# Stick-breaking logits: the second product from the high part of q alone, 64 rows in one of two row tiles

## The chip, the cores and the metric

One Trainium2 chip, one of its cores. The metric is the time of one execution of the program on the device, in microseconds; for the kernel before it is the median of three runs.

## What is computed

A decoder trunk of two layers over 512 tokens of width 1024. In each layer a SwiGLU half step, a mixing step (eight stick-breaking heads, eight forgetting heads, four memory heads, each branch gated), and another SwiGLU half step, each between RMS norms. The change touches the logits of the stick-breaking heads:

```python
def _stick_breaking_attention(q, k, v):          # 8 heads of 64, 512 tokens, blocks of 128 queries
    ...
        z = jnp.einsum('bhqd,bhkd->bhqk', qb, k).astype(jnp.float32) * scale
        mask = key_pos[None, :] < q_pos[:, None]
        log_beta = jax.nn.log_sigmoid(z)
        log_not = jnp.where(mask, log_beta - z, 0.0)
        log_between = lax.cumsum(log_not, axis=3, reverse=True) - log_not
        w = jnp.where(mask, jnp.exp(log_beta + log_between), 0.0)
        return jnp.einsum('bhqk,bhkd->bhqd', w.astype(v.dtype), v)
```

## The kernel before

Every product is done with operands that are split in two: a high part in TensorE's reduced 32-bit format (`F32R`) and a low part, the remainder. A full product takes three matmuls (`mm3`: high by high, high by low, low by high). `split(h, l, src)` writes the high part with ScalarE and the low part with VectorE.

The program writes its order out by hand. A queue `Q` holds the jobs of the dense products (projections, gates, branch outputs, each with its weights' loads), and `Q.weave` puts their steps between the parts of an attention head: a head is a generator that yields ("pe", us) after a part's matmuls and ("wait", us) where its next part should come only after so much other TensorE work.

A stick head is `stick_head` (L1174). Heads come in pairs: pair `p` has its q and k in one projection of 128 rows, head 0 on rows 0 to 63, head 1 on rows 64 to 127. `HEAD_ROWS` gives for each the rows `r` that are its own, the other half `ro`, and its index j:

```python
HEAD_ROWS = ((slice(0, HD), slice(HD, P), 0), (slice(HD, P), slice(0, HD), 1))
```

`proj` (L1374) makes the tiles. For q it is `[128, 2, 512]`: plane j has on rows `r` the high part of head j and on rows `ro` its low part. For the k of a stick head (`twice`) it is `[128, 4, 512]`: plane j has the high part of k on both halves, plane 2 + j the low part on both halves; GpSimd copies them from `r` to `ro` (L1390). So one matmul of 128 rows with plane j of both gives high by high plus low by high, and a second one, plane j of q with plane 2 + j of k, gives high by low plus low by low.

The head does this for query blocks i = 3, 2, 1, 0 of 128 queries, with 512, 384, 256 and 256 keys: block 3 in one PSUM bank, block 2 in another, blocks 1 and 0 together in a third (tag `z`, four banks). For each block both matmuls (L1183) stand one behind the other. Then ScalarE (L1188 to L1190: abs, exp, log) and VectorE (L1191, a scan at L1196, L1197) make the weights, ScalarE the last exponential (L1198). After a planned wait of 13 us of other TensorE work `transposed` (L1158) turns the weights with ten transposes and splits them, and `attend` (L1144) multiplies by v. There are 8 such heads in each of 2 layers.

Forgetting heads (`fox_head`, `fox_pre`) use the same `proj` with other shapes; their q stays `[128, 2, 512]`. Tiles of the tag `q` have two buffers.

Of the kernel before, what the change touches and what calls it, by code (L numbers as in the profile page):

```python
# [18 lines left out]
P = 128  # L19
# [4 lines left out]
def kernel(  # L24
# [38 lines left out]
    nc = tc.nc  # L63
    _, S, D = x.shape
    M = mem.shape[1]
    L = w_in.shape[0]
    NT = S // P
# [5 lines left out]
    HEAD_ROWS = ((slice(0, HD), slice(HD, P), 0), (slice(HD, P), slice(0, HD), 1))  # L73
# [25 lines left out]
    def tmp(name):  # L99
        return sb.tile([P, S], F32, tag="f32t", bufs=5, name=name)  # L100
# [3 lines left out]
    def stile(shape, tag, name, dt=F32R):  # L104
        return sb.tile(shape, dt, tag=tag, bufs=BUFS[tag], name=name)

    def blk(tag, name):
        return stile([P, 2, S], tag, name)

    def pbank(tag, name):  # L110
        return ps.tile([P, S], F32, tag=tag, bufs=4, name=name)
# [67 lines left out]
    def split(h_ap, l_ap, src, scale=None, later=False):  # L179

        if scale is None:
            both = [nc.scalar.copy(h_ap, src)]  # L182
            make = lambda: nc.vector.tensor_tensor(l_ap, src, h_ap.bitcast(F32), ALU.subtract)  # L183
        else:
            both = [nc.scalar.activation(h_ap, src, AF.Copy, scale=scale)]  # L185
            make = lambda: nc.vector.scalar_tensor_tensor(l_ap, src, scale, h_ap.bitcast(F32), ALU.mult, ALU.subtract)  # L186
        if later:
            return make
        both.append(make())
        if Q.pinned:  # L190
            for ins in both:
                tc.keep_in_program_order(ins)
        return both
# [16 lines left out]
    def gemm(pt, units, m, act, ks=None):  # L210

        last = sum(un.nk for un in units) - 1
        for un in units:
            for k in range(un.nk):
                kk = un.k0 + k
                if ks is not None and kk not in ks:
                    continue
                c = slice(m * P, (m + 1) * P)
                ah, al = act(kk)
                mm3(pt, un.h[:, k, c], un.l[:, k, c], ah, al, kk == 0, kk == last)  # L220
                yield 3 * pt.shape[1] * PE_US
# [914 lines left out]
    def attend(pv, j, vts, pj, tri, ot, name):  # L1136

        r, rl, _ = HEAD_ROWS[j]
        for kt in reversed(range(NT)):
            lo = QLO[kt]  # L1140
            v = vts[kt // 2][:, 2 * (kt % 2) + pj, 2 * j:2 * j + 2, :].rearrange("p e c -> p (e c)")
            for part in range(2):
                tc.keep_in_program_order(
                    nc.tensor.matmul(pv[:, lo:], v, tri_part(tri, part, kt, kt * P - lo), start=(kt == NT - 1 and part == 0),  # L1144
                                     stop=(kt == 0 and part == 1), skip_group_check=True))
        s = tmp("s" + name)
        nc.scalar.copy(s[r], pv[rl])
        nc.vector.tensor_tensor(s[r], pv[r], s[r], ALU.add)
        split(ot[r, 0], ot[r, 1], s[r])

    def transposed(ptile, name):

        tri = tri_tile("pt" + name)
        for kt in reversed(range(NT)):
            pt = pbank("z", f"pt{name}_{kt}")
            for i in range(kt, NT):
                tc.keep_in_program_order(
                    nc.tensor.transpose(pt[:, i * P:(i + 1) * P], ptile[i][:, kt * P:(kt + 1) * P], ident[:]))  # L1158
            split(tri_part(tri, 0, kt), tri_part(tri, 1, kt), pt[:, kt * P:].rearrange("p (a b) -> p a b", b=P))
        return tri  # L1160
# [12 lines left out]

    def stick_head(q, k, vts, pj, j, cut, ot, name):  # L1174

        ptile = {}
        for rows in ((3,), (2,), (1, 0)):
            pz = pbank("z", f"z{name}_{rows[0]}")
            w0 = (rows[0] + 1) * P
            for i in rows:  # L1180
                o = pz[:, (rows[0] - i) * 2 * P:][:, :max((i + 1) * P, 2 * P)]
                for kk in (j, 2 + j):
                    nc.tensor.matmul(o, q[:, j, i * P:(i + 1) * P], k[:, kk, :o.shape[1]], start=(i == rows[0] and kk == j),  # L1183
                                     stop=(kk == 2 + j), skip_group_check=True)
            w = w0 + (len(rows) - 1) * P
            zr, t = pz[:, :w], tmp(f"t{name}_{rows[0]}")

            nc.scalar.activation(t[:, :w], zr, AF.Abs)  # L1188
            nc.scalar.activation(t[:, :w], t[:, :w], AF.Exp, scale=-1.0)
            nc.scalar.activation(t[:, :w], t[:, :w], AF.Ln, bias=one_t[:])  # L1190
            nc.vector.scalar_tensor_tensor(t[:, :w], zr, 0.0, t[:, :w], ALU.max, ALU.add)  # L1191
            if len(rows) > 1:
                nc.vector.memset(t[:, w0 - 1:w0], 1e30)
            c1 = CUT if len(rows) > 1 else CUT - P
            back, fac = t[:, w - 1::-1], cut[:, c1 - w:c1][:, ::-1]
            nc.vector.tensor_tensor_scan(back, fac, back, 1e30, ALU.mult, ALU.add)  # L1196
            nc.vector.tensor_tensor(t[:, :w], zr, t[:, :w], ALU.subtract)  # L1197
            nc.scalar.activation(t[:, :w], t[:, :w], AF.Exp)  # L1198
            for i in rows:
                c = (rows[0] - i) * 2 * P  # L1200
                ptile[i] = t[:, c:c + (i + 1) * P]
        yield ("pe", 1.4)
        yield ("wait", W_SB0)
        wt = transposed(ptile, name)
        yield ("pe", 1.1)
        yield ("wait", W_SB1)
        attend(pbank("mm", "pv" + name), j, vts, pj, wt, ot, name)
        yield ("pe", 1.2)
# [120 lines left out]
    def mixing(l, src, ks, vs, rest, dst):  # L1329
# [5 lines left out]
        st, marks = {}, {}  # L1335
# [38 lines left out]
        def proj(key, un, scale):  # L1374
            nm = f"{key[0]}{l}_{key[1]}_{key[2]}"
            pt = pbank("mm", "p" + nm)
            yield from gemm(pt[:], [un], 0, act)
            if key[0] == "q":

                t = st[key] = blk("q", nm)  # L1380
                for r, ro, j in HEAD_ROWS:
                    split(t[r, j], t[ro, j], pt[r], scale=scale)
            else:

                twice = key[1] == 0
                t = st[key] = stile([P, 4 if twice else 3, S], "k", nm)
                for r, ro, j in HEAD_ROWS:
                    split(t[r, j], t[r, 2 + j if twice else 2], pt[r])
                    if twice:
                        nc.gpsimd.tensor_copy(t[ro, j::2], t[r, j::2])  # L1390
                    else:
                        nc.gpsimd.tensor_copy(t[ro, j], t[r, j])
# [12 lines left out]
        def project(br, p):  # L1405
            base = br * 1536
            marks["before", br, p] = len(Q.jobs)
            for x, off, scale in (("q", 0, 0.125), ("k", 512, None)):
                un1 = Unit(w_in[l], 0, ND, base + off + p * P, P, f"{x}{l}_{br}_{p}")
                marks[br, p] = Q.add([un1], lambda x=x, un1=un1, scale=scale: proj((x, br, p), un1, scale))  # L1410
                if (br, p, x) == (1, FOX[0], "k"):
                    Q.add([], lambda: forget_cumsum(l, st["fl"], st))
# [94 lines left out]
        def run():  # L1507
# [32 lines left out]
            def stick(p, j):  # L1540
                return stick_head(st["q", 0, p], st["k", 0, p], st["v", 0, p // 2], p % 2, j, st["cut"], st["o", 0][p],
                                  f"s{l}_{p}_{j}")
# [141 lines left out]
    for l in LAYERS:  # L1684
        i, mn = 3 * l, []
# [43 lines left out]
```

## Time and profile before

| | |
|---|---|
| median of three runs | 2349.4 us (2349.32 to 2351.5) |
| span of the profiled execution | 2349.9 us (first to last instruction; the page gives no other time of it) |
| TensorE products, busy | 2337.9 us (99%), 11623 matmuls |
| TensorE weight loads, busy | 1977.6 us (84%) |
| VectorE, ScalarE, GpSimd busy | 1799.9, 1506.5, 75.5 us |
| granted TensorE clock | 1.000 |
| stick heads | from 435.6 to 635.5 us, and from 1601.2 to 1800.9 us |

In the rows of the profile, PE is TensorE's products, PEld its weight loads, DVE is VectorE, ACT ScalarE, POOL GpSimd. L1183 is line 1183 of the kernel. A row of a timeline gives start, duration, engine, line, operation, what is written and read, the shape of the array used and of the moving operand; neighbours of one line are merged (x8), and the shape shown is the first one's. Matmuls are pipelined: the duration of one reaches over the start of the next, so distances are taken between starts.

### The profile page before, as it was taken

To read this page: it belongs to the slowest core of one execution; us is meant where nothing else is said; L and a number is where in the kernel's file an instruction comes from. 1 tells how busy PE (TensorE), PEld (TensorE's weight loads), DVE (VectorE), ACT (ScalarE), POOL (GpSimd) and SP (SyncE) were. 2 spreads that over 40 slices of the span, in tenths; PEclk is the share of its full clock that TensorE was granted. 3 is DMA by queue.
4 is the path that set the end of the run, shared out by engine and by line. 5 is a ranking of instruction groups with operands and counts; after the bars stand their busy time and mean duration, and the time that the engine had idled before them with its cause. 6 is when DMAs were issued, how large, how long until landed. Compare 5 with 4: busy or idle time off the path is not lost.

```text
span 2349.9 us, 30935 instructions
## 1 busy us (share of the span) xinstructions
PE 2337.9 (99%) x11623; PEld 1977.6 (84%) x11623; DVE 1799.9 (77%) x2359; ACT 1506.5 (64%) x2302; POOL 75.5 (3%) x134
## 2 busy tenths in 40 slices
PE   9999999999999999999999999999999999999998
PEld 7888888888888888888898888888888888888887
DVE  8877877577777688878798788766677766888785
ACT  6677465576766556775656775655777665567744
POOL 0000000000111000000000000000001100000000
PEclk9999999999999999999999999999999999999999
DMA  6667454223323554774646665532323235556744
GB/s 206 186 180 220 149 197 127 81 83 88 90 72 107 189 188 152 198 197 152 226 144 184 204 175 185 182 108 72 100 72 99 73 123 190 171 182 182 217 142 147
DMA packets 297849, 354.96 MB, mean 151 GB/s; under 512 B 78282, under 2 KB 189154, under 8 KB 297700
## 3 DMA queue, kind: packets, MB, share of 16 engines
q1 hardware_dynamic: 297604, 352.97, 49.0%
q8 instruction: 91, 1.49, 0.3%
q14 instruction: 58, 0.48, 0.1%
q0 software_dynamic: 96, 0.03, 0.0%
HBM read 319.39 MB, written 16.78 MB: 143 GB/s over the span
## 4 chain that ended last, share of the span: by engine, by line
PE 89%; DVE 3%; DMA 3%; ACT 3%; issue 2%; SPq 0%; DVEq 0%; ACTq 0%
PE pg L207 3%; PE pg L206 3%; PE pg L208 3%; PE pda L207 3%; PE pdc L207 3%; PE pda L206 3%; PE pda L208 3%; PE pdc L208 3%; PE pdc L206 3%; PE pq L207 1%; PE pq L206 1%; PE pk L207 1%; PE pb L208 1%; PE pk L208 1%; PE pq L208 1%
## 5 line engine op out<-in xcount | busy, mean ns | idle before, releaser
L206 PE MATMUL pg<-us_a,wh_wg 128*128 128x512 f32 x384 | 150.9, 393 | 0.0
L207 PE MATMUL pg<-us_a,wh_wg 128*128 128x512 f32 x384 | 149.7, 390 | 0.0
L208 PE MATMUL pg<-us_a,wl_wg 128*128 128x512 f32 x384 | 149.7, 390 | 0.0
L183 DVE TENSOR_TENSOR wl_da<-raw_da,wh_da 128x1024 fp32r<-128x1024 f32 x50 | 61.0, 1224 | 44.3 <-ACT wh_da L182 44.2
L183 DVE TENSOR_TENSOR wl_dc<-raw_dc,wh_dc 128x1024 fp32r<-128x1024 f32 x50 | 61.0, 1224 | 42.3 <-ACT wh_dc L182 42.3
L207 PE MATMUL pdc<-wl_dc,ahc 128*128 128x512 f32 x224 | 87.7, 391 | 0.0
L207 PE MATMUL pda<-wl_da,aha 128*128 128x512 f32 x224 | 87.6, 391 | 0.0
L208 PE MATMUL pdc<-wh_dc,alc 128*128 128x512 f32 x224 | 87.2, 389 | 0.0
L208 PE MATMUL pda<-wh_da,ala 128*128 128x512 f32 x224 | 87.2, 389 | 0.0
L206 PE MATMUL pdc<-wh_dc,ahc 128*128 128x512 f32 x224 | 86.5, 389 | 0.0
L206 PE MATMUL pda<-wh_da,aha 128*128 128x512 f32 x224 | 86.5, 389 | 0.0
L208 PEld LDWEIGHTS pg<-us_a,wl_wg 128*128 128x128 f32 x384 | 72.1, 188 | 15.1
L207 PEld LDWEIGHTS pg<-us_a,wh_wg 128*128 128x128 f32 x384 | 72.2, 188 | 14.1
L206 PEld LDWEIGHTS pg<-us_a,wh_wg 128*128 128x128 f32 x384 | 72.1, 188 | 14.1
L182 ACT CAST wh_da<-raw_da 128x1024 fp32r<-128x1024 f32 x50 | 52.3, 1051 | 45.6 <-PE pda L208 14.3
L182 ACT CAST wh_dc<-raw_dc 128x1024 fp32r<-128x1024 f32 x50 | 52.3, 1049 | 43.0 <-PE pdc L208 14.1
L186 DVE SCALAR_TENSOR_TENSOR wl_wg<-raw_wg,wh_wg 128x1024 fp32r<-128x1024 f32 x48 | 58.4, 1221 | 21.6 <-ACT wh_wg L185 21.6
L201 DVE SCALAR_TENSOR_TENSOR ga<-pg,bgate,ga 128x512 f32<-128x512 f32 x48 | 35.9, 748 | 48.4 <-ACT ga L200 48.4
L182 ACT CAST wh_uc<-raw_uc 128x1024 fp32r<-128x1024 f32 x44 | 46.3, 1053 | 38.4 <-PE pwc0g L208 9.1
L182 ACT CAST wh_ua<-raw_ua 128x1024 fp32r<-128x1024 f32 x44 | 46.2, 1053 | 31.7 <-PE pwa1g L208 8.6
L185 ACT ACTIVATE wh_wg<-raw_wg 128x1024 fp32r<-128x1024 f32 x48 | 50.6, 1057 | 24.5 <-PE pv L1119 11.7
L183 DVE TENSOR_TENSOR wl_uc<-raw_uc,wh_uc 128x1024 fp32r<-128x1024 f32 x44 | 53.8, 1222 | 16.2 <-ACT wh_uc L182 16.0
(643 smaller groups left out, 8015.9 us busy)
## 6 DMA issues: line engine op xcount, KB each, us to landing
raw_da<-in_ffn_w_down_dram SPq DMA_DIRECT2D x66, 512.0 KB, 4.8
raw_dc<-in_ffn_w_down_dram SPq DMA_DIRECT2D x66, 512.0 KB, 4.3
raw_ga<-in_ffn_w_gate_dram SPq DMA_DIRECT2D x52, 512.0 KB, 4.5
raw_ua<-in_ffn_w_up_dram SPq DMA_DIRECT2D x52, 512.0 KB, 4.5
raw_gc<-in_ffn_w_gate_dram SPq DMA_DIRECT2D x52, 512.0 KB, 4.2
raw_uc<-in_ffn_w_up_dram SPq DMA_DIRECT2D x52, 512.0 KB, 4.0
raw_wg<-in_w_gate_dram SPq DMA_DIRECT2D x48, 512.0 KB, 3.6
raw_wo<-in_w_out_dram SPq DMA_DIRECT2D x24, 512.0 KB, 3.4
```

The source lines that it names most:

```text
L182: both = [nc.scalar.copy(h_ap, src)]
L183: make = lambda: nc.vector.tensor_tensor(l_ap, src, h_ap.bitcast(F32), ALU.subtract)
L185: both = [nc.scalar.activation(h_ap, src, AF.Copy, scale=scale)]
L186: make = lambda: nc.vector.scalar_tensor_tensor(l_ap, src, scale, h_ap.bitcast(F32), ALU.mult, ALU.subtract)
L201: nc.vector.scalar_tensor_tensor(t, z, minus, t, ALU.max, ALU.add)
L206: nc.tensor.matmul(pt, lh, rh, start=start, stop=False, skip_group_check=free)
L207: nc.tensor.matmul(pt, lh, rl, start=False, stop=False, skip_group_check=free)
L208: nc.tensor.matmul(pt, ll, rh, start=False, stop=stop, skip_group_check=free)
```

## The change

The second matmul takes only the 64 rows with the high part of q, so low by low is no longer computed. For block 3 these are the head's own rows `r` of plane j; for blocks 2, 1 and 0 they are the rows `ro`, the other half, from a new third plane of q into which GpSimd copies the high part. A matmul of 64 rows occupies one of the two halves (row tiles) of the array. All four first matmuls of a head now come before the four second ones, and all eight are held in this order. The kernel's scratch for software DMAs is set to 4096 bytes a partition; the q tiles take 2048 bytes a partition more for each of two buffers.

```diff
     def stick_head(q, k, vts, pj, j, cut, ot, name):
 
-        ptile = {}
-        for rows in ((3,), (2,), (1, 0)):
-            pz = pbank("z", f"z{name}_{rows[0]}")
-            w0 = (rows[0] + 1) * P
+        ptile, pzs = {}, {}
+        r, ro, _ = HEAD_ROWS[j]
+        ROWS = ((3,), (2,), (1, 0))
+        out_ = lambda rows, i: pzs[rows][:, (rows[0] - i) * 2 * P:][:, :max((i + 1) * P, 2 * P)]
+        for rows in ROWS:
+            pzs[rows] = pbank("z", f"z{name}_{rows[0]}")
             for i in rows:
-                o = pz[:, (rows[0] - i) * 2 * P:][:, :max((i + 1) * P, 2 * P)]
-                for kk in (j, 2 + j):
-                    nc.tensor.matmul(o, q[:, j, i * P:(i + 1) * P], k[:, kk, :o.shape[1]], start=(i == rows[0] and kk == j),
-                                     stop=(kk == 2 + j), skip_group_check=True)
+                o = out_(rows, i)
+                tc.keep_in_program_order(
+                    nc.tensor.matmul(o, q[:, j, i * P:(i + 1) * P], k[:, j, :o.shape[1]], start=i == rows[0], stop=False,
+                                     skip_group_check=True))
+        for rows in ROWS:
+            for i in rows:
+                o, (on, e) = out_(rows, i), (r, j) if i == NT - 1 else (ro, 2)
+                tc.keep_in_program_order(
+                    nc.tensor.matmul(o, q[on, e, i * P:(i + 1) * P], k[on, 2 + j, :o.shape[1]], start=False, stop=True,
+                                     skip_group_check=True))
+        for rows in ROWS:
+            pz, w0 = pzs[rows], (rows[0] + 1) * P
             w = w0 + (len(rows) - 1) * P
             zr, t = pz[:, :w], tmp(f"t{name}_{rows[0]}")
...
             if key[0] == "q":
 
-                t = st[key] = blk("q", nm)
+                twice = key[1] == 0
+                t = st[key] = stile([P, 3 if twice else 2, S], "q", nm)
                 for r, ro, j in HEAD_ROWS:
                     split(t[r, j], t[ro, j], pt[r], scale=scale)
+                    if twice:
+                        nc.gpsimd.tensor_copy(t[ro, 2], t[r, j])
...
-    nc = _bacc.Bacc("TRN2", target_bir_lowering=False, num_devices=1)
+    nc = _bacc.Bacc("TRN2", target_bir_lowering=False, num_devices=1, dynamic_dma_scratch_size=4096)
```

## The prediction

> **What bounds the kernel now.** I read the page first: busy time, then the chain that ended last.
>
> ```profile
> span 2349.9 us, 30935 instructions
> PE 2337.9 (99%) x11623; PEld 1977.6 (84%) x11623; DVE 1799.9 (77%) x2359; ACT 1506.5 (64%) x2302; POOL 75.5 (3%) x134
> PE 89%; DVE 3%; DMA 3%; ACT 3%; issue 2%; SPq 0%; DVEq 0%; ACTq 0%
> ```
>
> TensorE is never free and nine tenths of the last chain is its own work. The share is a mean, so I asked for the busy time by stage; the stick-breaking heads lie in these two stretches (columns: length, then busy time and instruction count of each engine).
>
> ```profile
> 420.00:590.00 170.00, 170.00 (x942) 148.67 (x941) 114.30 (x173) 113.57 (x200) 12.63 (x19) 1.00 0.30 84
> 1585.00:1785.00 200.00, 200.00 (x1086) 173.99 (x1086) 137.44 (x207) 140.07 (x247) 13.09 (x21) 1.00 0.30 86
> ```
>
> PE has no hole there at all, at full granted clock. So a nanosecond taken from PE's queue in a stick head is a nanosecond off the end, and one added is added; the other engines matter only if they make PE wait. The answer on the tile `zs` says how much work is touched:
>
> ```profile
> L1183 PE MATMUL zs<-k,q x128: 278/310/397, 435.6 to 1778.4; 128*128 128x256 f32 x64, 128*128 128x512 f32 x32, 128*128 128x384 f32 x32
> ```
>
> 128 products are 16 heads of 8: four first ones and four second ones, of 512, 384, 256 and 256 columns. Their durations (278 to 397 ns) are pipelined; what counts is the distance between starts. I take it from the timeline of PE in a forgetting head, where the lines alternate and each start is seen, and check it on a whole stick head.
>
> ```profile
> 636.51 0.39 PE L1235 MATMUL zf<-qk 104*128 104x512 f32 x1
> 636.74 0.34 PE L1234 MATMUL zf<-k,q 128*128 128x384 f32 x1
> 636.92 0.34 PE L1235 MATMUL zf<-qk 104*128 104x384 f32 x1
> 637.09 0.28 PE L1234 MATMUL zf<-k,q 128*128 128x256 f32 x1
> 637.21 0.29 PE L1235 MATMUL zf<-qk 104*128 104x256 f32 x1
> ...
> 435.37 0.39 PE L208 MATMUL pq<-us_a,wl_q 128*128 128x512 f32 x1
> 435.60 1.45 PE L1183 MATMUL zs<-k,q 128*128 128x512 f32 x8
> 436.88 0.40 PE L206 MATMUL pq<-us_a,wh_q 128*128 128x512 f32 x1
> ```
>
> A slot is 0.23 us for 512 columns, 0.175 for 384 (636.74 to 637.09 is two), 0.12 for 256. Eight products: 2 x (0.23 + 0.175 + 0.12 + 0.12) = 1.29; the head above takes 436.88 - 435.60 = 1.28. The second products alone are half, 0.64 us a head, 10.2 us in the kernel: what is at stake at most.
>
> **The change, part by part.**
>
> *Fewer rows.* The columns stay, and the slots above don't follow rows (104 rows of 512 columns take 0.23 as well). So 64 rows alone save nothing. What can save is that row 3's product (512 columns) lies on one half of the array and rows 2, 1, 0 on the other: if both halves work at once, the four take as long as the longer side. No row shows two halves at work. Bounds: they take turns, saving 0; or row 3 vanishes wholly behind the others, 0.175 + 0.12 + 0.12 = 0.415 instead of 0.64, saving 0.227. Between them stands the weight load: each product brings 128 columns of weights of its own, and where products are short, loads set the pace, as in the transposes:
>
> ```profile
> 578.52 1.25 PE L1158 MATMUL pts<-ident,ts 128*128 128x128 f32 x10
> 579.61 0.60 PE L1313 MATMUL pfl<-ident,fl 128*8 128x128 f32 x4
> ```
>
> Ten in 1.09 us, 0.109 each, though 128 columns would need only half a 256-column slot. If loads go one after the other, row 2's product starts 0.109 behind row 3's, and the four end at 0.109 + 0.175 + 0.12 + 0.12 = 0.524: saving 0.118. I take this one, as the only row on loads supports it, and keep 0 and 0.227 as ends.
>
> *Changing the array's shape, twice a head:* from 128 rows to 64 after the four first products, and back for the work that follows. Before, no stick head has it. The nearest rows are the two small transposes of vectors, 8 and 48 rows, amid a dense stream (first PE's products, then its weight loads):
>
> ```profile
> 312.09 0.39 PE L208 MATMUL pda<-wh_da,ala 128*128 128x512 f32 x1
> 312.40 0.22 PE L126 MATMUL vecs_t<-ident,vecs 8*128 8x8 f32 x1
> 312.56 0.26 PE L127 MATMUL vecs_t<-ident,vecs 48*128 48x48 f32 x1
> 312.75 0.50 PE L206 MATMUL pda<-wh_da,hida 128*128 128x512 f32 x1
> 313.08 0.39 PE L207 MATMUL pda<-wl_da,hida 128*128 128x512 f32 x1
> ```
> ```profile
> 312.40 0.13 PEld L126 LDWEIGHTS vecs_t<-ident,vecs 8*128 8x128 f32 x1 [0.35 <-issue]
> 312.56 0.13 PEld L127 LDWEIGHTS vecs_t<-ident,vecs 48*128 48x128 f32 x1
> 312.75 0.19 PEld L206 LDWEIGHTS pda<-wh_da,hida 128*128 128x128 f32 x1
> 312.85 0.19 PEld L207 LDWEIGHTS pda<-wl_da,hida 128*128 128x128 f32 x1
> ```
>
> In 128-row shape 312.09 to 313.08 would be 0.23 + 0.109 + 0.109 + 0.23 = 0.67; it took 0.99. The 0.32 more over three changes of shape (128 to 8 to 48 to 128) are 0.107 each, 0.21 a head: the value I take, being a measured sum. It can be dearer: a load normally runs under the product before it, and here the first one starts 0.08 after the slot of 312.09 is over (312.32), the last one 0.19 after the 48-row load (0.109 of it load, 0.02 the 48 columns, so 0.06 waiting). Waits of 0.08 and 0.06 with two loads of 0.109 laid bare are 0.36 a head, the upper end. The lower end is 0, should the changes hide. The Trainium skill, "TensorEngine Tiling (Array Packing)", Key Properties, says that a change of tiling mode (not merely of tile) drains TensorE; the rows above agree with 0.06 to 0.08 us of waiting. By that rule alone, with every load hidden, two changes cost 0.14 and the sum would be 16 x (0.14 - 0.118) = +0.4 us; by the measured excess it is the following.
>
> *Sum:* 0.21 - 0.118 = +0.09 us a head, x16 = +1.5 us.
>
> *Order.* All first products now precede the second ones, so row 3's logits are complete not after two slots but after four, a change of shape and its second product: 0.46 becomes 0.64 + 0.15 + 0.23, some 0.55 us later; rows 1 and 0 finish about when they did. ScalarE waits for them, then the softplus chain, then PE's transposes. The tightest head of the layer, in the timelines of PE and ScalarE and the list of PE's waits:
>
> ```profile
> 587.48 1.44 PE L1183 MATMUL zs<-k,q 128*128 128x512 f32 x8
> 590.95 0.60 ACT L1188 ACTIVATE ts<-zs 128x512 f32<-128x512 f32 x1
> 603.03 0.53 ACT L1198 ACTIVATE ts<-ts 128x384 f32<-128x384 f32 x1
> 603.06 1.53 PE L1158 MATMUL pts<-ident,ts 128*128 128x128 f32 x10
> PEld pts L1158 <- ACT ts L1198: 0.3, 1, 0.3
> ```
>
> Its logits were done by 588.8 (587.48 + 1.28), and ScalarE came to them only at 590.95, so 0.55 later changes nothing; the last exponential ends inside the transposes (603.56), a wait of 0.3, the only one of these transposes in the run. Cost 0, at most 0.3 more in that head of each layer.
>
> *Copies.* q gets a third plane, two POOL copies of 64x512 for each of 4 pairs and 2 layers: 16 in all. The same shape of copy from q exists, and the copies of k stand in the same queue behind them:
>
> ```profile
> L1215 POOL CAST qk<-q 64x512 fp32r<-64x512 f32 x16 | 9.7, 607 | 43.4 <-DVE ts L1196 24.1 <-PE zf L1235 19.3
> 422.39 1.04 POOL L1390 CAST k<-k 64x1024 fp32r<-64x1024 f32 x1 [0.24 <-DVE k L183]
> ```
>
> 16 x 0.61 = 9.7 us on an engine that is 3% busy. The pair with the least room is the first: its last copy of k ends at 423.4 and its head starts at 435.60, 12 us later, so the 1.2 us by which two more copies can delay it cost 0; without that cover it would be 1.2 us a pair. The clears of the transposed tile queued behind them have the same room. More SBUF for q, less scratch for three early software DMAs: nothing waits for either, 0.
>
> The trace's own span, 2349.9, lies 0.5 above the median run (2349.4) and inside the runs' spread (2349.32 to 2351.5); I add to the median: 2349.4 + 1.5 = 2350.9. About 0.2% (4.7 us) is what a measurement here can tell from no change.
>
> **Rivals.**
>
> *A: both halves run at once and the changes of shape hide.* Row 3's product vanishes: 16 x 0.227 = 3.6 us, 2345.8. For it: separate banks, separate rows, one pair of changes a head. Against it: the rows at 312. The Trainium skill, "TensorE: Matmul & The Clock Gate", Part 3, gives a pack as one matmul's time and 4 ns for each further tile, which is this rival's overlap (no run here shows it); it prices no change of mode.
>
> *B (slower): the halves take turns, and each change lays its load bare.* Saving 0, price 0.36: 16 x 0.36 = +5.8, 2355.2. It decides against the change from a net 0.29 us a head (4.7 / 16) on. For it: the loads at 312.40 and 312.75 begin only once the stream has stopped; against it, the measured excess per change of 0.107.
>
> *C: the change doesn't do what it says:* 64 rows run as 128 do, with neither overlap nor change of shape, as the 104-row products do (0.23 for 512). 2349.4.
>
> *D: the order on other queues shifts* and makes or removes a hole elsewhere. PE's busy time leaves 12 us of holes in the whole span, outside these stages; a few us either way.
>
> **How the numbers follow.** Forecast (overlap paid back by the two changes, -1 to +4): 0.50, all but 0.02 of it within 0.2%. A 0.20: -3.6 is within 0.2%, 0.04 beyond it. B 0.12, of which 0.11 slower by over 0.2%. C 0.10. D 0.08: 0.04 faster, 0.03 slower. So faster 0.08, slower 0.16, same 0.76. The range goes from A's 2345.8 to B's 2355.2, both ends being bounds of the unknown prices.
>
> **What would show it.** Right: in the timeline, the second products with 64 rows start in pairs closer than 0.2 us; the load ahead of row 3's starts after the slot before it ends, as does the next 128-row load; head start to the next work about 1.37 us instead of 1.28. A would show 1.05, B 1.64, C 1.28. Transposes that wait for ScalarE in more than one head a layer would make the order's cost wrong; PE waiting for POOL would make the copies' cost wrong.

## The result and the profile after

The change made the kernel slower by about a quarter of a per cent: 2356.59 us (median of 14 runs, 2355.01 to 2359.0) against 2351.47 (14 runs, 2349.32 to 2353.03), ratio 1.0023 with a 95% interval of 1.0015 to 1.0031. In a second measurement, against new runs of the kernel before, it was 2354.0 against 2348.18, ratio 1.0024 (1.0015 to 1.0033). That is some 5 to 6 us, in the direction to which the prediction gave 0.16. The time lies beyond its range (2345.8 to 2355.2).

Two things make up the distance to the forecast of 2350.9: the change cost 5.1 us where 1.5 was forecast, and the kernel before, with more runs, has its median at 2351.47, 2.1 above the 2349.4 to which the forecast was added. The intervals of the ratios here are some 2 us wide to either side, so single differences of about 1 us between kernels can't be told from none.

The page of the changed kernel, its first lines and the chain's shares:

```profile
span 2354.9 us, 30956 instructions
PE 2341.2 (99%) x11623; PEld 1976.5 (84%) x11623; DVE 1800.3 (76%) x2359; ACT 1507.6 (64%) x2302; POOL 89.5 (4%) x150
PE 89%; DVE 3%; DMA 3%; ACT 3%; issue 2%; SPq 0%; DVEq 0%; ACTq 0%
```

The span grew by 5.0 us (2349.9 to 2354.9) with the same number of matmuls. Nothing in the shares shows where. The busy time by stage does: the two stretches of the prediction and the one that follows the first, after the change, then the one that follows the first as it was before:

```profile
420.00:590.00 170.00, 169.78 (x934) 146.81 (x933) 114.22 (x172) 112.25 (x198) 15.68 (x24) 1.00 0.29 84
590.00:620.00 30.00, 28.87 (x138) 23.81 (x136) 20.77 (x30) 24.69 (x43) 1.72 (x4) 1.00 0.26 79
1585.00:1785.00 200.00, 198.57 (x1079) 171.06 (x1079) 135.27 (x205) 136.26 (x242) 17.39 (x27) 1.00 0.29 84
```
```profile
590.00:620.00 30.00, 29.94 (x143) 24.97 (x142) 22.92 (x32) 26.47 (x47) 0.46 (x3) 1.00 0.32 97
```

PE has holes in the stick stages now, 0.2, 1.1 and 1.4 us, where before two of them had none and the third 0.06. The waits of the weight loads name them (columns: total, times, longest):

```profile
PEld pts L1158 <- ACT ts L1208: 3.7, 4, 1.4
```

Four waits of the transposes for the last exponential of a head, 3.7 us, against one of 0.3 before. They lie in the sixth and seventh head of each layer. Compared by the starts of PE's products, they put back what follows by 0.38, 1.07, 0.44 and 1.31 us, 3.2 in all. The other part lies in the heads. One head before and the same head after, in PE's timeline, then the weight loads after:

```profile
515.41 1.44 PE L1183 MATMUL zs<-k,q 128*128 128x512 f32 x8
516.70 0.40 PE L206 MATMUL pg<-us_a,wh_wg 128*128 128x512 f32 x1
516.93 0.39 PE L207 MATMUL pg<-us_a,wh_wg 128*128 128x512 f32 x1
```
```profile
515.83 0.80 PE L1185 MATMUL zs<-k,q 128*128 128x512 f32 x4
516.56 0.67 PE L1191 MATMUL zs<-k,q 64*128 64x512 f32 x4
517.16 0.50 PE L206 MATMUL pg<-us_a,wh_wg 128*128 128x512 f32 x1
517.49 0.40 PE L207 MATMUL pg<-us_a,wh_wg 128*128 128x512 f32 x1
```
```profile
516.56 0.47 PEld L1191 LDWEIGHTS zs<-k,q 64*128 64x128 f32 x4
517.16 0.19 PEld L206 LDWEIGHTS pg<-us_a,wh_wg 128*128 128x128 f32 x1
517.27 0.19 PEld L207 LDWEIGHTS pg<-us_a,wh_wg 128*128 128x128 f32 x1
```

From the first product to the second one of the work that follows: 1.52 us before, 1.66 after, 0.14 more. The next few products lie a little further apart as well; six products on, a head has added 0.15 to 0.18, on the mean 0.17, or 2.7 us in all. Read the steps: the four first products end their slots at 515.83 + 0.64 = 516.47, but the first load of 64 rows starts at 516.56 (a wait of 0.09). A load that isn't hidden takes 0.11 by the rows above (517.16 to 517.27), 0.108 by the single records. From 516.56 to 517.16 there are 0.60 us, in which one load (0.108), the slots of blocks 2, 1 and 0 (0.415) and a second wait of 0.09 fill all, so block 3's 0.23 has vanished. The next product is followed after 0.33 instead of 0.23, since its load runs in the open (517.16 to 517.27).

So 5.0 = 2.7 (heads) + 3.4 (transposes, 3.7 - 0.3) - 1.1 elsewhere, most of it in waits outside these stages, where both kernels do the same work. What each is due to had to be tried.

### The profile page after: what moved, and what is told of

Same layout as the page of the kernel before. It is cut to its first block, busy times and chain, and to the rows that moved or that the text cites. A ratio compares the mean times of both kernels' runs of the same rounds, so it can differ in the third digit from the quotient of the medians.

```text
span 2354.9 us, 30956 instructions
## 1 busy us (share of the span) xinstructions
PE 2341.2 (99%) x11623; PEld 1976.5 (84%) x11623; DVE 1800.3 (76%) x2359; ACT 1507.6 (64%) x2302; POOL 89.5 (4%) x150
## 4 chain that ended last, share of the span: by engine, by line
PE 89%; DVE 3%; DMA 3%; ACT 3%; issue 2%; SPq 0%; DVEq 0%; ACTq 0%
PE pg L206 3%; PE pg L207 3%; PE pg L208 3%; PE pda L207 3%; PE pda L206 3%; PE pda L208 3%; PE pdc L207 3%; PE pdc L208 3%; PE pdc L206 3%; PE pb L208 1%; PE pb L206 1%; PE pb L207 1%; PE pq L206 1%; PE pq L207 1%; PE pk L206 1%
```

## The experiments

The theory after seeing this: two changes of shape cost 0.20 us each and the overlap gives back 0.227, and apart from that the later logits have changed the order of instructions in ScalarE's and VectorE's queues, which is laid down when the program is built. The rivals: GpSimd's copies disturb VectorE and ScalarE and so cause the waits; or the prediction's prices hold and something else is lost.

**The order alone.** All first products, then all second ones, each of 128 rows; no third plane, no copies, the scratch as before.

```diff
-                o, (on, e) = out_(rows, i), (r, j) if i == NT - 1 else (ro, 2)
+                o, (on, e) = out_(rows, i), (slice(0, P), j)
```

> The changed order of the products alone: all four first ones, then the four second ones, each of 128 rows as before, so no change of the array's shape, no overlap, no copies on GpSimd. Theory: of the 5 us that the change costs, 16 x 0.17 = 2.7 us lie in the heads (two changes of shape at 0.20 each, less 0.227 of overlap) and about 3.4 us in transposes of the sixth and seventh head of each layer that wait for a last exponential, because the later logits of block 3 changed the order of ScalarE's and VectorE's queues. So here the heads take 1.28 us again, those two waits stay, and the kernel is 2 to 3.8 us slower than before. Rival (the waits come from GpSimd's copies, which disturb VectorE): no waits beyond the one of 0.3 us, time as before within 0.6 us.

Measured: 2351.85 against 2348.32, ratio 1.0015 (1.0006 to 1.0024): 3.5 us slower with not one row saved or shape changed. A head, and the waits of the weight loads:

```profile
513.43 0.81 PE L1185 MATMUL zs<-k,q 128*128 128x512 f32 x4
514.07 0.81 PE L1191 MATMUL zs<-k,q 128*128 128x512 f32 x4
514.72 0.40 PE L206 MATMUL pg<-us_a,wh_wg 128*128 128x512 f32 x1
514.95 0.40 PE L207 MATMUL pg<-us_a,wh_wg 128*128 128x512 f32 x1
```
```profile
PEld pts L1158 <- ACT ts L1208: 4.1, 4, 1.6
```

The head takes 1.29 us as before; the four waits are there. The order of instructions on ScalarE and VectorE in this kernel is that of the change, instruction for instruction, and differs from that of before. What this does is seen in the changed kernel's seventh head (VectorE, ScalarE, then PE):

```profile
603.86 0.55 DVE L1207 TENSOR_TENSOR ts<-zs,ts 128x384 f32<-128x384 f32 x1
```
```profile
604.73 1.05 ACT L182 CAST wh_k<-raw_k 128x1024 fp32r<-128x1024 f32 x1 [0.93 <-DMA raw_k<-in_w_in_dram]
605.69 0.52 ACT L1208 ACTIVATE ts<-ts 128x384 f32<-128x384 f32 x1
```
```profile
604.64 0.49 PE L1158 MATMUL pts<-ident,ts 128*128 128x128 f32 x3
606.26 0.98 PE L1158 MATMUL pts<-ident,ts 128*128 128x128 f32 x7 [1.13 <-ACT ts L1208]
```

VectorE has the last exponential's input ready at 604.41. ScalarE stands idle then: next in its queue is the cast of the next k weights, which waits 0.93 us for its DMA, and the exponential is behind it. Before, the exponential (603.03) stood ahead of that cast:

```profile
604.08 1.05 ACT L182 CAST wh_k<-raw_k 128x1024 fp32r<-128x1024 f32 x1 [0.52 <-DMA raw_k<-in_w_in_dram]
```

Lateness itself is not the cause here: VectorE has that input ready 15.5 us after the head's first product, before and after alike (602.99 - 587.48 and 604.41 - 588.89). In the sixth head it is VectorE's queue (first before, then after):

```profile
573.88 0.95 DVE L1196 TENSOR_TENSOR_SCAN ts<-cut,ts 128x384 f32<-128x384 f32 x1
576.96 1.23 DVE L183 TENSOR_TENSOR wl_wb<-raw_wb,wh_wb 128x1024 fp32r<-128x1024 f32 x1 [0.54 <-ACT wh_wb L182]
```
```profile
576.89 1.22 DVE L183 TENSOR_TENSOR wl_wb<-raw_wb,wh_wb 128x1024 fp32r<-128x1024 f32 x1 [0.40 <-ACT wh_wb L182]
578.03 0.95 DVE L1206 TENSOR_TENSOR_SCAN ts<-cut,ts 128x384 f32<-128x384 f32 x1
```

The head's last scan now stands behind the low part of a weight tile, which waits for ScalarE's cast of that weight, and that cast waited 0.70 us for its DMA. The same two heads of the second layer show the same two orders.

**The copies alone.** The kernel before with the third plane, its 16 copies and the smaller scratch; nothing reads the plane.

```diff
-                t = st[key] = blk("q", nm)
+                twice = key[1] == 0
+                t = st[key] = stile([P, 3 if twice else 2, S], "q", nm)
...
+                    if twice:
+                        nc.gpsimd.tensor_copy(t[ro, 2], t[r, j])
...
```

> The kernel before with the third plane of q, its 16 copies on GpSimd and the smaller scratch, and nothing else: no product reads the plane. Theory: time as before within 0.6 us, transposes wait as before. Rival (copies disturb VectorE and ScalarE): about 3.4 us slower, with waits of 0.4 and 1.1 us at the transposes of the sixth and seventh head of each layer.

Measured: 2347.92 against 2348.32, ratio 0.9998 (0.9989 to 1.0007). The transposes wait 0.5 us once. The copies cost nothing that shows (at most 1.6 us by the interval), as predicted, and the rival, which asked for 3.4 us and four waits, falls.

**One half only.** The change with all second products on rows `r`; no third plane, no copies, the scratch as before.

```diff
-                o, (on, e) = out_(rows, i), (r, j) if i == NT - 1 else (ro, 2)
+                o, (on, e) = out_(rows, i), (r, j)
```

> The change with all second products on the head's own half of the array, so none can lie beside another; no third plane, no copies. Theory: the overlap of 0.227 us a head is gone, 16 x 0.227 = 3.6 us slower than the change, 8.5 to 9.5 us slower than before; block 2's product starts 0.23 us after block 3's instead of 0.003. Rival (the prediction's prices: 0.21 us a head for the two changes of shape, overlap only 0.118, and the rest of the loss from the copies): 16 x 0.21 = 3.4 us slower than before.

Measured: 2357.08 against 2348.32, ratio 1.0038 (1.0025 to 1.0051), 8.8 us, within the 8.5 to 9.5 expected. In PE's timeline the four products of 64 rows now take 0.84 us where the change took 0.60:

```profile
516.35 0.91 PE L1191 MATMUL zs<-k,q 64*128 64x512 f32 x4
517.19 0.50 PE L206 MATMUL pg<-us_a,wh_wg 128*128 128x512 f32 x1
```

The difference of 0.24 is about block 3's slot (0.23): on two halves it is hidden wholly.

**Four pairs of changes a head.** The order of before, the second products with 64 rows on the head's own half.

```diff
-                    nc.tensor.matmul(o, q[:, j, i * P:(i + 1) * P], k[:, kk, :o.shape[1]], start=(i == rows[0] and kk == j),
-                                     stop=(kk == 2 + j), skip_group_check=True)
+                    on = slice(0, P) if kk == j else HEAD_ROWS[j][0]
+                    tc.keep_in_program_order(
+                        nc.tensor.matmul(o, q[on, j, i * P:(i + 1) * P], k[on, kk, :o.shape[1]],
+                                         start=(i == rows[0] and kk == j), stop=(kk == 2 + j), skip_group_check=True))
```

> The order of before, each block's second product behind its first, but the second one with 64 rows on the head's own half: four pairs of changes of shape in a head instead of one, nothing beside anything, no copies, ScalarE's and VectorE's queues in the order of before. Theory: 4 x 0.40 = 1.6 us a head, 16 x 1.6 = 25.6 us slower than before. Rival (the prediction's 0.107 for one change): 4 x 0.21 x 16 = 13.7 us slower. If a change were cheaper where a short product lies between two of them: in between.

Measured: 2373.39 against 2348.32, ratio 1.0107 (1.0093 to 1.0121): 25.1 us, 25.6 expected. Over 16 heads and 8 changes a head that is 0.196 us for one change.

```profile
518.11 2.81 PE L1185 MATMUL zs<-k,q 128*128 128x512 f32 x8
520.85 0.50 PE L206 MATMUL pg<-us_a,wh_wg 128*128 128x512 f32 x1
521.19 0.40 PE L207 MATMUL pg<-us_a,wh_wg 128*128 128x512 f32 x1
```

Eight products in 2.74 us instead of 1.29 (516.70 - 515.41), and 0.11 more from the next product to the one after it.

**Taking the waits away, first try.** The planned wait between logits and transposes at 15 us instead of 13 (`W_SB0`), in the change, in the kernel before and in the order alone.

> The change, with the planned wait between a stick head's logits and its transposes raised from 13 to 15 us of other TensorE work. Theory: the transposes of the sixth and seventh head of each layer come after their last exponential again, the waits on ScalarE (3.7 us in the change's trace) fall below 0.6, and what is left is the price in the heads, 16 x 0.17 = 2.7 us: 2 to 3.4 us slower than before. Rival (the later queue order costs PE elsewhere too, wherever the transposes stand): still 4.5 to 5.5 us slower.

> The control: the kernel before with the same planned wait of 15 us. Theory: its one wait of 0.3 us at the transposes goes, nothing else moves: 0 to 0.8 us faster than before. Rival: the longer wait shifts other work of the planner and costs something by itself (over 0.8 us slower).

> The changed order of the products with 128 rows, with the planned wait of 15 us. Theory: without the waits at the transposes the order costs nothing: within 0.6 us of the control (the kernel before with 15 us), against 3.5 us at 13. Rival: 2 us or more slower than the control.

Measured, against 2348.02: the change 2355.98, ratio 1.0033 (1.0021 to 1.0046); the kernel before 2351.49, ratio 1.0014 (1.0004 to 1.0023); the order alone 2352.69, ratio 1.0019 (1.001 to 1.0028). All three expectations missed. The control was to be up to 0.8 us faster; 15 us everywhere costs it 3.5 us by itself, as its rival had it, so the change, 8.0 us slower than before, fits neither of its two ranges. The transposes of stick heads no longer wait in any of the three, but PE waits in other places; the control's:

```profile
PEld pvs L1144 <- DVE pts L183: 0.9, 2, 0.5
PEld pb L207 <- DVE o L183: 0.8, 2, 0.4
PEld pvs L1144 <- issue: 0.6, 2, 0.3
```

Against it the order alone is 1.2 us slower (at 13 us of planned wait it was 3.5; 0.6 at most was expected, 2 by its rival) and the change 4.5. That the waits go is shown; as a measure of what is left it is blunt, since the longer wait lays ScalarE's and VectorE's queues anew too.

**The change and the order alone on one chip; the waits taken away in two heads alone.** For the latter only the sixth and seventh head of each layer wait longer:

```diff
-        yield ("wait", W_SB0)
+        yield ("wait", W_SB0 + (1.6 if name[-3:] in ("2_1", "3_0") else 0.0))
```

> The change itself, beside the changed order alone on the same chip. Theory: 5 to 6 us slower than before, and 16 x 0.165 = 2.6 us slower than the changed order alone (2 to 3.2), since queues and waits are alike and only the heads differ. Rival (the heads' price is smaller and part of it is lost twice, once in the heads and once as longer waits): 1 to 1.8 us slower than the changed order alone.

> The changed order alone, 128 rows, again on this chip. Theory: 2.8 to 4 us slower than before, all of it at the four transposes that wait for ScalarE. Rival as in its first run: none that its first run left; this is the partner of the change on one chip.

> The change with 1.6 us more of planned wait in the two tight heads of each layer alone (the sixth and seventh), 13 us in the others. Theory: the waits at their transposes go (from 3.7 us to under 0.8), with less disturbance than 15 us everywhere made: 2.2 to 3.2 us slower than its control with the same two waits. Rival (the lost time only moves to another wait): 4 us or more slower than the control.

> The control: the kernel before with the same 1.6 us more in the same two heads of each layer. Theory: within 0.8 us of before; if it is faster, it is the version that beats both. Rival: as 15 us everywhere did, it costs 1.5 us or more by other waits.

Measured, against 2348.18: the change 2354.0, ratio 1.0024 (1.0015 to 1.0033); the order alone 2351.74, 1.0015 (1.0006 to 1.0024); the change with the two longer waits 2351.5, 1.0013 (1.0004 to 1.0022); the control with them 2348.04, 1.0 (0.9991 to 1.0009). So the change is 2.3 us above the order alone, where 2.6 were expected, and the order alone 3.6 above before. The waits for ScalarE at these transposes (the change, the order alone):

```profile
PEld pts L1158 <- ACT ts L1208: 3.6, 4, 1.5
PEld pts L1158 <- ACT ts L1208: 3.7, 4, 1.3
```

With the two longer waits that row is gone from the list, and the change loses 3.5 us to its control instead of 5.8 to the kernel before. That is above what was expected for the heads (2.2 to 3.2) and below the rival's 4: taking the waits away gave back 2.4 us, where the order alone costs 3.6. In the two profiles, 3.4 us apart, the heads account for 0.17 us each again, 2.7; the remaining 0.7 lies in small steps elsewhere and is within the intervals. These longer waits also lay the queues anew, so this run measures the sum and does not single out one queue. The control is no faster than the kernel before, so no version here beats it.

## Why the prediction was wrong

It forecast 2350.9, in the range 2345.8 to 2355.2, and no measurable change. Of the miss, 2.1 us lie in the median of the kernel before and say nothing on the mechanism; the rest lies in the steps:

- **What bounds the kernel** held: two kernels came within 0.5 us of sums made of PE's time alone. Four pairs cost 25.1 against 64 x 0.40 = 25.6; one half 8.8 against 16 x 0.40 and 2.6 more of waits at the transposes (2.9 in its trace, 0.3 before), 9.0.
- **The overlap was too small in the sum:** 0.118 us a head taken, 0.24 measured (0.84 - 0.60, the one-half kernel against the change), about its upper end of 0.227. The weight loads were assumed to follow one another. In the single records the starts of block 3's and block 2's products lie 3 to 4 ns apart in all 16 heads, and block 1's product starts 0.28 behind them: one load and one slot of block 2 (0.108 + 0.175), with no room for a second load. So both halves load at once, which is rival A's overlap. The 4 ns for a further tile that the Trainium skill gives ("TensorE: Matmul & The Clock Gate", Part 3) agrees with these 3 to 4 ns.
- **The change of shape was too cheap:** 0.107 each taken, 0.196 to 0.2 measured; the pair costs 0.40, above even the upper end of 0.36. The measured excess at the vectors' transposes was the wrong price to carry over: there the sum for 128-row shape already held two slots of 0.109 that are nothing but loads, so the excess of 0.32 over three changes left two of three bare loads out. With them it is (0.32 + 2 x 0.109) / 3 = 0.18 a change, near what was measured. Amid products of 256 to 512 columns, whose loads are hidden in the kernel before, each change shows its wait of 0.09 and a whole load of 0.108. The rows for this were quoted; the choice between the two readings was wrong. The rule that a change of mode drains the array (Trainium skill, "TensorEngine Tiling (Array Packing)", Key Properties) agrees with the wait of 0.09. That wait is less than half of the price measured here.
- The two errors partly cancelled: +0.09 a head forecast, +0.17 measured, 2.7 us instead of 1.5.
- **The order was held to cost 0, at most 0.3 more in one head of each layer. This is the step that failed:** 3.4 us of waits, two heads in each layer, 3.5 us in time when the order was run alone. The prediction's own sign for this, transposes that wait for ScalarE in more than one head a layer, came. The reasoning looked at when the logits would be there and who had slack, with every queue in the order that it had. But the order of those queues is laid down when the program is built, and with the new order of products other work came ahead of the chain. (That the build goes by estimated times, and moved this work since block 3's product ends later, is the likely reason; no run here tests it.) In the seventh head the later logits delayed nothing: VectorE's last result came 15.5 us after the first product as before. What delayed the exponential was a weight cast that had come to stand ahead of it and waited for its DMA; in the sixth head it was the low part of a weight ahead of VectorE's scan. The prediction had a shift of order as rival D, "the order on other queues shifts", but outside the stick stages and with 0.08.
- **Copies and scratch cost 0:** right to within the interval of the copies alone, although a copy took 0.75 us on the mean instead of the 0.61 taken (12.0 us on GpSimd, line 1395 of the changed kernel).

Rival B gave nearly the right cost, 5.8 us, by luck: its change of shape at 0.36 was close, but its halves take turns, and here they do not; the waits at the transposes, which it lacks, fill the difference.

The trade can be closed with an estimate from these numbers. The second products of a head are 0.64 us; a perfect split over two halves saves 0.32, less than the 0.40 that going into the other shape and back costs. So no packing of one head's second products would pay. Two heads sharing one pair of changes would need six logit banks where there are four; that was not tried.

## What to carry to other kernels

Here two row tiles overlapped wholly, but in a dense stream of 128-row products a visit to 64-row shape cost 0.40 us, whatever was moved: two waits of 0.09 and two loads that nothing hides. Weigh that against half the time of the products moved, and batch until it is small. And when the order on one engine is changed, compare the order in the other engines' queues before and after, not only the slack: where queues are ordered at build time, a new order on one engine can put the cast of a weight that hasn't landed ahead of the chain that TensorE needs next.

## What the runs showed of the hardware that was not expected

- Two products of 64 rows on different halves of the array, in different banks, started 3 to 4 ns apart, and their loads ran at the same time: the four second products took 0.60 us on two halves and 0.84 on one, waits and one bare load included in both.
- In the four-pairs kernel a change between 128 and 64 rows cost the same, to within some 0.01 us, in both directions and with products of 256, 384 or 512 columns on either side: 0.08 to 0.10 of waiting and 0.108 of load.
